# Sliding windows by DMA on one Trainium2 core: a twelfth staged batch, 32 KB packets everywhere, and engine groups set a quarter turn apart

## The chip, the cores and the metric

The kernel runs on one core of one Trainium2 chip. It uses no compute engine for its work: it only moves data with the core's 16 DMA engines. The metric is the device time of one execution in microseconds (us); lower is better. Times are medians of several runs. Ratios are the mean time of one kernel's fast runs over the mean of the other's of the same rounds on the same chip, so a ratio is not quite the ratio of the medians quoted beside it.

## The reference, cut to what matters

```python
batch, length, dim = (32, 4096, 256)      # x: float32, 134 MB
window_size, stride = 64, 32              # so n_windows = 127
for i in range(n_windows):
    start = i * stride
    result[:, i] = x[:, start:start + window_size].copy()
```

Call 32 rows of `x` (32 KB) a *block*. A batch has 128 blocks, and window `i` is block `i` followed by block `i+1`. Nearly every block is therefore written twice. The output is 266.3 MB.

## The kernel before

There are two ways to make a batch of output.

- *Direct*: one DMA copies from `x` in HBM to the output in HBM. Each output byte goes through a DMA engine once, and costs HBM one read and one write (by the page below, 174.83 MB direct counted twice and 138.41 MB staged counted once make 488.07 MB, and HBM read and wrote 488.04 MB).
- *Staged*: a batch's 128 blocks are loaded into SBUF, one block per partition, and stored from there twice. The load is an extra pass through the DMA engines (4.19 MB per batch), but HBM is read only half as often.

The kernel before stages every third batch (11 of 32). Direct work goes out on the queue of the sync engine (`ring_d`, q1 in the profile), staged work on the queue of the scalar engine (`ring_s`, q10), and leftovers of the direct batches (15 windows each, the *edges*) at the end on the software ring of GpSimd (`ring_r`, q0).

```python
DIRECT, IN, OUT = 32768, 16384, 16384       # largest packet, in bytes
...
    def load(self, q, g):                   # class Staging; 6 tiles in SBUF
        ...
        parts = [(k, 4, 32, 1) for k in range(4)] if g == 0 else [(0, step, n, step)]
        for rows in parts:                  # (first partition, step, how many, unit)
            self.issue(self.c.load(q, self.tiles[i], b, c, rows), self.loaded[i])

    def store(self, q, g):
        ...
        parts, end = [((0, step, n, step), 0), ((0, step, n, step), 1)], []
...
    staged = [*range(1, B, 3)]
...
        for i, (b, w) in enumerate(sixteens):       # direct work, 16 windows at a time
            ...                                     # one or two DMAs, by a running share
            count(c.windows(ring_d, b, w, 16), sem)
        ring_r.wait_ge(near, 16)                    # direct queue nearly done
        for b, w, n in edges:
            for k in (b - 1, b + 1):
                if k in place and b != last:
                    st.wait_stored(ring_r, place[k])
            count(c.windows(ring_r, b, w, n), rest)
        count(c.columns(ring_r, last, 116, 9), rest)
```

One DMA is spread over the engines, and each engine takes packets from the queues in turn: the packet records name no engine, but chained end to start, wherever only one chain fits, 99% of the packets in 60-560 us of this kernel's trace are of another queue than the packet before them. What matters is the *turn*: a data packet is one, and so is the four-byte packet at the end of each DMA that counts its semaphore (the 204 direct DMAs of this kernel left 3264 of these in the trace, 16 each). The share of the direct queue is thus set by how many turns in a queue carry data and how long the packets are.

## Time and profile before

| | before |
|---|---|
| time, median of 3 runs | 744.34 us |
| span of the profiled execution | 749.4 us |
| bytes through the DMA engines | 313.26 MB |
| HBM read and written | 220.95 + 267.09 MB |

These are lines of the page of the kernel before: the busy share of the DMA engines in 40 slices (in tenths), what they moved in each slice, the packets, and for each queue its packets, MB and share of the engines' span.

```profile
...
DMA  8999999999999999999999999999999999999996
GB/s 360 401 427 429 427 429 428 434 423 418 420 424 423 418 424 415 422 427 427 414 427 417 429 432 429 430 422 430 429 423 421 423 421 419 425 426 423 431 409 262
DMA packets 18290, 313.26 MB, mean 418 GB/s; under 512 B 4336, under 2 KB 4336, under 8 KB 4528
...
q1 hardware_dynamic: 8016, 154.32, 48.8%
q10 hardware_dynamic: 9104, 138.41, 44.0%
q0 software_dynamic: 1168, 20.51, 6.5%
...
HBM read 220.95 MB, written 267.09 MB: 651 GB/s over the span
...
```

The engines are busy from the second slice to the last but one. The time can only fall if fewer bytes pass, if packets get faster, or if start and end get shorter. The next lines are stretches of the same trace (columns: stretch, its length, GpSimd's busy time, clock, DMA share, GB/s): batches being loaded, then two stretches in which they are stored, then the hand-over from the direct queue to the software ring.

```profile
...
30.00:120.00 90.00, 0.00 (x0) 1.00 1.01 427
150.00:400.00 250.00, 0.00 (x0) 1.00 1.00 422
530.00:650.00 120.00, 0.00 (x0) 1.00 1.01 422
650.00:660.00 10.00, 5.61 (x10) 1.00 0.99 421
...
```

Loading runs at 427 GB/s and storing at 422. The trace's record of each packet shows how far that is from the best: a 32 KB packet takes 1213 ns in the median (1211 at the least), which is called undisturbed below. The mean of the direct queue in this trace is 1236 ns. Staged 16 KB packets take 611 ns undisturbed and 624 on average. Packets that follow each other overlap by 3 to 4 ns in the records, so undisturbed 32 KB packets start 1209 ns apart. That is 27.1 GB/s per engine and 433.6 GB/s for 16, the best rate in what follows.

### The profile page before, as it was taken

The page shows a single profiled execution, that of the slowest core. Times are in us where ns is not written, and L with a number is a line of the kernel's source. Part 1 is how long each engine was busy: PE and PEld are TensorE (multiplying, and loading weights), DVE is VectorE, ACT ScalarE, POOL GpSimd, SP SyncE. Part 2 cuts the span into 40 slices and gives each one's busy share as a digit, 9 for nine tenths or more (in the row PEclk, how much of TensorE's full clock was granted, in tenths as well). Part 3 has the DMA queues.
Part 4 walks back from the last instruction along what each step waited for, and adds up shares of the span by engine and source line. Part 5 has one row for each costly group of instructions (what it writes and reads, how often), then busy time and mean ns, then how long its engine had stood idle before and what let it go on. Part 6 is the DMA issues. An engine that isn't in the chain of part 4 may idle for free.

```text
span 749.4 us, 322 instructions
## 1 busy us (share of the span) xinstructions
POOL 12.8 (2%) x26
## 2 busy tenths in 40 slices
POOL 0000000000000000000000000000000000040100
DMA  8999999999999999999999999999999999999996
GB/s 360 401 427 429 427 429 428 434 423 418 420 424 423 418 424 415 422 427 427 414 427 417 429 432 429 430 422 430 429 423 421 423 421 419 425 426 423 431 409 262
DMA packets 18290, 313.26 MB, mean 418 GB/s; under 512 B 4336, under 2 KB 4336, under 8 KB 4528
## 3 DMA queue, kind: packets, MB, share of 16 engines
q1 hardware_dynamic: 8016, 154.32, 48.8%
q10 hardware_dynamic: 9104, 138.41, 44.0%
q0 software_dynamic: 1168, 20.51, 6.5%
q14 instruction: 2, 0.02, 0.0%
HBM read 220.95 MB, written 267.09 MB: 651 GB/s over the span
## 4 chain that ended last, share of the span: by engine, by line
another core or an unknown queue 92%; POOL 2%; issue 0%; POOLq 0%; SPq 0%
POOL out_dram L34 2%; POOL out_dram L44 0%; POOLq L236 0%; SPq L172 0%; POOLq L114 0%
## 5 line engine op out<-in xcount | busy, mean ns | idle before, releaser
L34 POOL DMA_DIRECT2D out_dram<-in_x_dram x21 | 12.0, 576 | 691.3 <-DMA out_dram<-in_x_dram 654.0
L44 POOL DMA_DIRECT2D out_dram<-in_x_dram x1 | 0.6, 581 | 0.0
L222 POOL MEMSET const-float32-0.0<- 128x1 f32 x1 | 0.1, 98 | 0.2 <-issue 0.2
L222 POOL MEMSET const-bfloat16-1.0<- 128x1 bf16 x1 | 0.1, 101 | 0.0
L222 POOL MEMSET const-float32-1.0<- 128x1 f32 x1 | 0.1, 98 | 0.0
L222 POOL MEMSET const-uint8-127<- 128x1 uint8 x1 | 0.1, 98 | 0.0
## 6 DMA issues: line engine op xcount, KB each, us to landing
out_dram<-in_x_dram SPq DMA_DIRECT2D x92, 1024.0 KB, 100.7
out_dram<-xb ACTq DMA_DIRECT2D x21, 4096.0 KB, 139.7
out_dram<-in_x_dram SPq DMA_DIRECT2D x110, 512.0 KB, 90.3
xb<-in_x_dram ACTq DMA_DIRECT2D x10, 4096.0 KB, 131.4
out_dram<-in_x_dram POOLq DMA_DIRECT2D x20, 960.0 KB, 38.5
xb<-in_x_dram ACTq DMA_DIRECT2D x4, 1024.0 KB, 15.7
out_dram<-xb ACTq DMA_DIRECT2D x2, 1024.0 KB, 113.4
out_dram<-xb ACTq DMA_DIRECT2D x4, 512.0 KB, 96.9
```

The costliest lines, as they stand in the source:

```text
L34: return q.dma_start(out=self.oap((b * self.nw + w0) * 2 + h, [[2 * blk, n], row]), in_=self.xap(b * self.nb + w0 + h, [[blk, n], row]), m ...
L44: return q.dma_start(out=self.oap((b * self.nw + w0) * 2, [[part, 16], [2 * self.blk, n], row]), in_=self.xap(b * self.nb + w0, [[part, 16 ...
L222: nc = _bacc.Bacc("TRN2", target_bir_lowering=False, num_devices=1)
```

## The change

The intent, in the words it came with: "As few long packets: 12 staged batches, all 32 KB, share 0.52 throughout; groups of 4 engines set a quarter turn apart by the software ring".

```diff
-DIRECT, IN, OUT = 32768, 16384, 16384
+DIRECT, IN, OUT, REST = 32768, 32768, 32768, 32768
...
+    def quarters(self, q, b, w0, p0, n):      # 4 windows, meant for 4 engines; n quarters of a turn each
+    def many(self, q, b, w0, n, half):        # 16 engines x n packets of 32 KB, one semaphore
...
-        parts = [(k, 4, 32, 1) for k in range(4)] if g == 0 else [(0, step, n, step)]
-        for rows in parts:
+        for rows in self.split(2):
...
+    def split(self, parts):
+        return [(k, parts, 128 // parts, 1) for k in range(parts)]
...
-        parts, end = [((0, step, n, step), 0), ((0, step, n, step), 1)], []
+        split = self.split(8 if g >= len(self.items) - 4 else 2)
+        parts, end = [(rows, half) for half in (0, 1) for rows in split], []
...
-    staged = [*range(1, B, 3)]
+    staged = [0, 3, 6, 9, 11, 14, 17, 20, 22, 25, 28, 31]
...
+        for k in range(3):
+            count(c.quarters(ring_r, apart[0], apart[1] + 4 * k, 0, 3 - k), rest)
         st.run(ring_s)
...
+        for i, (b, w, n, half) in enumerate(main):
+            count(c.many(ring_d, b, w, n, half), near if i == len(main) - 2 else done)
...
         ring_r.wait_ge(near, 16)
+        for k, p in ((3, 0), (0, 3), (1, 2), (2, 1)):
+            count(c.quarters(ring_r, apart[0], apart[1] + 4 * k, p, 4 - p), rest)
```

`split(2)` is two DMAs of 64 rows (every second partition): 4 data packets and a semaphore packet per engine. A direct `many` is 7 data packets and one semaphore packet. So of two queues that take turns the direct one has 0.875 / (0.875 + 0.8) = 0.52 of the bytes. `split(8)`, used for the stores of the last four batches, is eight DMAs of 16 rows, every eighth partition: one data packet per engine and one semaphore packet.

More of the change, by code (lines that the diff above doesn't have):

```diff
@@ L37, in windows @@
             max_dma_last_dim=piece,
+        )
+    def quarters(self, q, b, w0, p0, n):
+        part = self.blk // 4
+        at = p0 * 2 * part
+        dims = [[n * part, 2], [1, n * part]]
+        return q.dma_start(
+            out=bass.AP(self.out.tensor, self.oap((b * self.nw + w0) * 2, dims).offset + at, [[2 * self.blk, 4], *dims]),
+            in_=bass.AP(self.x.tensor, self.xap(b * self.nb + w0, dims).offset + at, [[self.blk, 4], *dims]),
+            max_dma_last_dim=4 * n * part,
+        )
+    def many(self, q, b, w0, n, half):
+        return q.dma_start(
+            out=self.oap((b * self.nw + w0) * 2 + half, [[2 * self.blk, 16], [32 * self.blk, n], [1, self.blk]]),
+            in_=self.xap(b * self.nb + w0 + half, [[self.blk, 16], [16 * self.blk, n], [1, self.blk]]),
         )
@@ L87, in load @@
         i = g % len(self.tiles)
-        b, c, n = self.items[g]
         if self.count[self.stored[i]]:
             q.wait_ge(self.stored[i], self.count[self.stored[i]])
-        step = 128 // n
-        parts = [(k, 4, 32, 1) for k in range(4)] if g == 0 else [(0, step, n, step)]
-        for rows in parts:
-            self.issue(self.c.load(q, self.tiles[i], b, c, rows), self.loaded[i])
+        for rows in self.split(2):
+            self.issue(self.c.load(q, self.tiles[i], *self.items[g], rows), self.loaded[i])
         self.after_load[g] = self.count[self.loaded[i]]
+    def split(self, parts):
+        return [(k, parts, 128 // parts, 1) for k in range(parts)]
     def store(self, q, g):
         i = g % len(self.tiles)
-        b, c, n = self.items[g]
         q.wait_ge(self.loaded[i], self.after_load[g])
-        step = 128 // n
-        parts, end = [((0, step, n, step), 0), ((0, step, n, step), 1)], []
+        split = self.split(8 if g >= len(self.items) - 4 else 2)
+        parts, end = [(rows, half) for half in (0, 1) for rows in split], []
         if g == len(self.items) - 1:
-            parts = [((0, 1, 128, 1), 1), ((0, 1, 32, 1), 0)]
-            end = [(96, 1, 32, 1)] + [(32 + k, 4, 16, 1) for k in range(4)]
+            parts = [(rows, 1) for rows in split] + [(split[0], 0)]
+            end = split[1:]
         for rows, half in parts:
-            self.issue(self.c.store(q, self.tiles[i], b, c, rows, half), self.stored[i])
+            self.issue(self.c.store(q, self.tiles[i], *self.items[g], rows, half), self.stored[i])
         for rows in end:
-            self.issue(self.c.store(q, self.tiles[i], b, c, rows, 0), self.ended)
+            self.issue(self.c.store(q, self.tiles[i], *self.items[g], rows, 0), self.ended)
         self.after_store[g] = self.count[self.stored[i]]
@@ L140 @@
     c = Copier(x, out, B, L, D, W, S, n_win)
-    staged = [*range(1, B, 3)]
-    items = [(b, -1 if b == B - 1 else 0, c.nb) for b in staged]
-    place = {b: g for g, (b, _, n) in enumerate(items) if n == c.nb}
+    staged = [0, 3, 6, 9, 11, 14, 17, 20, 22, 25, 28, 31]
+    items = [(b, 1 if b == 0 else -1 if b == B - 1 else 0) for b in staged]
+    place = {b: g for g, b in enumerate(staged)}
     direct = [b for b in range(B) if b not in staged]
@@ L157, in count @@
         total[sem] += 16
-    sixteens = []
+    main, edges, singles = [], [], [(B - 1, c.nw - 1, 1)]
+    if 0 in staged:
+        singles.append((0, 0, 0))
+    last = B - 2
     for b in direct:
-        w = 15 if b - 1 in staged else 0
-        sixteens += [(b, w + 16 * j) for j in range((c.nw - w) // 16)]
-    singles = [(B - 1, c.nw - 1, 1)]
-    edges = [(b, 0 if b - 1 in staged else 112, 15) for b in direct[:-1]]
-    last = B - 2
-    edges.append((last, 112, 4))
-    first_loads, loads, stores = 6 * 17, 5 * 17, 6 * 34
-    turns = share = 0
+        before, behind = b - 1 in staged, b + 1 in staged
+        w = 15 if before and (not behind or b == last) else 8 if before else 0
+        if b == last:
+            w = 0
+        main += [(b, w + 16 * j, min(7, 7 - j), half) for j in range(0, 7, 7) for half in (0, 1)]
+        if b == last:
+            edges.append((b, 112, 3))
+        elif before and behind:
+            edges += [(b, 0, 8), (b, 120, 7)]
+        else:
+            edges.append((b, 0 if before else 112, 15))
+    b, w, n, half = main.pop()
+    main += [(b, w, n - 1, half), (b, w + 16 * (n - 1), 1, half)]
+    apart = main[-2][:2]
+    main = [(b, w + 16, n - 1, half) if (b, w) == apart else (b, w, n, half) for b, w, n, half in main]
     with tc.tile_critical():
+        for k in range(3):
+            count(c.quarters(ring_r, apart[0], apart[1] + 4 * k, 0, 3 - k), rest)
         st.run(ring_s)
-        for i, (b, w) in enumerate(sixteens):
-            sem = near if i == len(sixteens) - 2 else done
-            second = turns - first_loads - stores
-            loading = turns < first_loads or 0 <= second < loads
-            share += 120 if turns < 16 or -8 <= second < 16 else 90 if loading else 18
-            if share >= 120:
-                share -= 120
-                turns += 4
-                count(c.windows(ring_d, b, w, 16, 0), done)
-                count(c.windows(ring_d, b, w, 16, 1), sem)
-            else:
-                turns += 3
-                count(c.windows(ring_d, b, w, 16), sem)
-            if i == len(sixteens) // 2:
+        for i, (b, w, n, half) in enumerate(main):
+            count(c.many(ring_d, b, w, n, half), near if i == len(main) - 2 else done)
+            if i == len(main) // 2:
                 for b, w, half in singles:
@@ L196 @@
                     st.wait_stored(ring_r, place[k])
-            count(c.windows(ring_r, b, w, n), rest)
-        count(c.columns(ring_r, last, 116, 9), rest)
+            count(c.windows(ring_r, b, w, n, None, REST), rest)
+        count(c.columns(ring_r, last, 115, 10), rest)
         st.wait_stored(ring_d, place[B - 1])
```

## The prediction

> **What bounds the kernel now.** The 16 DMA engines. The page's DMA row is at 9 in 38 of 40 slices, the stretches from 20 to 720 us show a DMA share of 1.00, and the three queues together hold 99.3% of the engines' span (48.8 + 44.0 + 6.5). So the time is bytes per engine over its best rate, plus a cost per packet, plus slow packets, start and tail.
>
> By the trace's packet records a 32 KB packet takes 1213 ns at best and 1236 on average (direct queue); a staged 16 KB packet 611 at best, 624 on average.  [...] Summed over the best time of their kind, packets lose about 15 us per engine (6.6 direct, 7.0 staged, 1.3 software ring). About 0.5 to 0.9% while batches are loaded (about 40-120 and 415-520 us, direct share of the bytes 0.53), 2.2% while they are stored (150-400 and 530-650 us, share 0.57), 2.5 to 3% in the last 80 us, more in the first 30 us, where all engines go in step (up to 16 direct packets at once). Within the store stretches the loss rises with the direct share: about 1% or less at 0.52, over 4% above 0.62. Direct packets load HBM twice[...].
>
> **What the change does.**
> - Adds one staged batch in place of a direct one: 4.19 MB more through the engines (about 313.3 to 317.5 MB, +1.36%). [...]+9.7 us, wholly on the critical path.
> - Removes half of the staged packets: 872 data packets per engine become about 606. With fewer semaphore packets about 2 us saved (packets overlap by 3-4 ns).
> - Moves the direct share of the store stretches from 0.57 to 0.52. Estimate from the loss by share: 2.2% to about 0.8% over roughly 350 us, 4 to 5 us saved; the load stretches stay.
> - But the last four batches are stored one packet per two turns, so the direct share there is about 0.64, then 0.57 beside the software ring: 100 to 150 us where 2 to 3% stay.
> - The quarter turns break the step at the start; jitter breaks it after about 50 us anyway: at most 2 us.
>
> Sum: about +2 us; if steady share and phases take nearly all the loss away, about -6. The profiled run is some 7 us longer than the timed ones, so part of the loss may exist only there. Middle: 742.5 us.
>
> **What would show it.** After: about 317.5 MB, near 9,700 data packets, direct and staged packets all 32 KB; store stretches with mean packets nearer 1213 ns (about 1222) and 425 to 430 GB/s instead of 422; engines in direct packets at once near 8, with little spread from 20 us on; last 100 us unchanged or worse.
>
> **What would make it wrong.** Lower: loss vanishes everywhere (floor about 737). Higher: [...]equal packets keep engines in step for the whole run; engines end unevenly because the pieces are longer.
>
> Predicted 742.5 us, 735 to 751 in 8 of 10; faster by over 2% 0.02, within 2% 0.94, slower 0.04.

The sum came to about +2 us: +9.7 for the bytes (4.19 MB at the 433.6 GB/s measured above give the same), less 2 for packets, less 4 to 5 for the share, less at most 2 for the quarter turns. The middle, 742.5 us, lies between this +2 and the -6 of the better case. Of the "jitter" the trace of before shows this much: the standard deviation of the number of engines in direct packets at once falls from 6.9 in the first 10 us to 3.3 in 50-60 us.

## More of the kernel before

Last, lines of the timeline (columns: start, time until the last of them, queue, line, operation, names, how many). They show the end: when the direct queue is nearly done, the software ring sends 18 edges at once, and three more after it has waited for stores.

```profile
...
431.72 222.98 ACTq L63 DMA_DIRECT2D out_dram<-xb  x15
654.39 10.26 POOL L34 DMA_DIRECT2D out_dram<-in_x_dram  x18 [653.95 <-DMA out_dram<-in_x_dram]
702.01 1.72 POOL L34 DMA_DIRECT2D out_dram<-in_x_dram  x3 [37.36 <-DMA out_dram<-xb]
...
```

## The result, and the profile after

| | before | after |
|---|---|---|
| time, median of 5 runs | 744.34 us (743.5 to 745.25) | 763.93 us (762.73 to 765.84) |
| ratio, 95% interval | | 1.0265 (1.0247 to 1.0283) |
| span of the profiled execution | 749.4 us | 760.9 us |
| bytes through the DMA engines | 313.26 MB | 317.54 MB |
| HBM read and written | 220.95 + 267.09 MB | 216.86 + 267.19 MB |

The change is slower by 2.65%, outside the predicted range. The lines of its page that answer to those of before:

```profile
...
DMA  8999999999999999999999999999999999999995
GB/s 365 436 427 434 434 431 427 429 438 432 434 427 439 429 429 434 436 436 427 427 427 431 434 438 429 433 432 429 434 436 407 412 413 415 266 402 403 425 409 245
DMA packets 13313, 317.54 MB, mean 417 GB/s; under 512 B 3400, under 2 KB 3400, under 8 KB 3624
...
q10 hardware_dynamic: 6528, 151.00, 47.6%
q1 hardware_dynamic: 5216, 145.95, 44.8%
q0 software_dynamic: 1568, 20.58, 6.6%
...
HBM read 216.86 MB, written 267.19 MB: 636 GB/s over the span
...
```

Up to slice 30 (570 us) this looks better than before: all slices from the second on are at 427 to 439 GB/s. Then come four slices at 407 to 415, one at 266, and five that reach 425 at most. Yet the DMA share stays at 9 tenths: the engines are not idle there, their packets are slow. The stretches (columns as above):

```profile
...
30.00:560.00 530.00, 0.00 (x0) 1.00 1.00 432
560.00:640.00 80.00, 0.00 (x0) 1.00 1.00 415
640.00:680.00 40.00, 13.32 (x23) 1.00 0.99 333
646.00:658.00 12.00, 10.72 (x19) 1.00 1.01 265
...
```

The steady part runs at 432 GB/s. From 560 us it is 415, and around 650 us it is 265 GB/s with all engines busy. The timeline lines of the end:

```profile
...
386.99 277.66 ACTq L81 DMA_DIRECT2D out_dram<-xb  x72
644.55 2.40 POOL L45 DMA_DIRECT2D out_dram<-in_x_dram  x4 [641.05 <-DMA out_dram<-in_x_dram]
646.96 9.76 POOL L34 DMA_DIRECT2D out_dram<-in_x_dram  x17
669.03 1.16 POOL L34 DMA_DIRECT2D out_dram<-in_x_dram  x2 [12.31 <-DMA out_dram<-xb]
712.50 1.71 POOL L34 DMA_DIRECT2D out_dram<-in_x_dram  x3 [42.31 <-DMA out_dram<-xb]
...
```

From 386.99 us on the staged stores are issued. At 644.55 the software ring begins, with the four closing quarter pieces first, then 17 edges. Between 646 and 658 us the packet records show almost only staged packets in flight, with means of 1.6 to 2.7 us in two-microsecond steps, up to 2.2 times the undisturbed 1.21 us.

**Two traces of one chip.** The first profile of before was long (its profiled run took 751.2 us, its timed runs 744 to 745). Profiled again in two later jobs, on two chips, its spans were 744.1 and 743.8; yet another chip took 752 us for the same kernel (below). So the account is made from two traces of one chip, taken side by side: before with a span of 743.8 us, the change with 762.8. First the kernel before, then the change:

```profile
...
0.00:30.00 30.00, 0.20 (x4) 1.00 0.93 385
30.00:560.00 530.00, 0.00 (x0) 1.00 1.01 428
560.00:640.00 80.00, 0.00 (x0) 1.00 1.01 427
640.00:680.00 40.00, 10.26 (x18) 1.00 1.01 429
680.00:720.00 40.00, 2.30 (x4) 1.00 1.01 425
...
```

```profile
...
0.00:30.00 30.00, 2.14 (x7) 1.00 0.94 389
30.00:560.00 530.00, 0.00 (x0) 1.00 1.00 432
560.00:640.00 80.00, 0.00 (x0) 1.00 1.00 410
640.00:680.00 40.00, 13.34 (x23) 1.00 0.99 337
680.00:720.00 40.00, 2.27 (x4) 1.00 1.01 415
...
```

"Lost" below is the length of a stretch less the time that the bytes in it (by the packet records) take at 433.6 GB/s, the best rate measured above. The expectations count it against a rate 0.4% higher, so their losses are larger by 0.4% of the stretch (120-560 us: 11.1 and 3.5 us there, 9.5 and 1.9 here). Share is the direct part of the bytes.

| stretch, us | before: share, lost | change: share, lost | difference |
|---|---|---|---|
| all bytes at the best rate | 722.3 us | 732.2 us | +9.9 |
| 0-30 | 0.55, 3.7 | 0.50, 3.6 | -0.1 |
| 30-560 | 0.56, 7.4 | 0.52, 2.2 | -5.2 |
| 560-640 | 0.58, 1.3 | 0.62, 4.1 | +2.8 |
| 640-680 | 0.51, 0.5 | 0.36, 8.9 | +8.4 |
| 680-720 | 0.58, 0.9 | 0.53, 2.1 | +1.2 |
| 720 to the end | 0.63, 7.7 | 0.55, 9.7 | +2.0 |
| sum | | | +19.0 |

The steady part does what it was built for. Its gain is half of the added bytes, and from 560 us on nearly three times the gain is lost (14.4 us). The gain has two parts. In 30-560 us the packets' time over the best of their kind (1213 and 611 ns) fell from 5.1 to 1.5 us per engine, so 3.6 us come from fewer slow packets; the other 1.6 us come from fewer packets (817 per engine before, 526 after, semaphore packets included).

### The profile page after: what moved, and what is told of

It reads as the page before. It is cut to its first block, busy times and chain, and to the rows that moved or that the text cites. A ratio compares the mean times of both kernels' runs of the same rounds, so it can differ in the third digit from the quotient of the medians.

```text
span 760.9 us, 252 instructions
## 1 busy us (share of the span) xinstructions
POOL 17.7 (2%) x34
## 2 busy tenths in 40 slices
DMA packets 13313, 317.54 MB, mean 417 GB/s; under 512 B 3400, under 2 KB 3400, under 8 KB 3624
## 3 DMA queue, kind: packets, MB, share of 16 engines
HBM read 216.86 MB, written 267.19 MB: 636 GB/s over the span
## 4 chain that ended last, share of the span: by engine, by line
another core or an unknown queue 91%; POOL 2%; issue 0%; PEldq 0%
POOL out_dram L34 1%; POOL out_dram L45 1%; POOL out_dram L62 0%; PEldq L261 0%
## 5 line engine op out<-in xcount | busy, mean ns | idle before, releaser
L45 POOL DMA_DIRECT2D out_dram<-in_x_dram x7 | 4.3, 622 | 642.2 <-DMA out_dram<-in_x_dram 641.0
L34 POOL DMA_DIRECT2D out_dram<-in_x_dram x22 | 12.6, 577 | 54.6 <-DMA out_dram<-xb 54.6
L62 POOL DMA_DIRECT2D out_dram<-in_x_dram x1 | 0.6, 553 | 0.0
```

The costliest lines, as they stand in the source:

```text
L34: return q.dma_start(out=self.oap((b * self.nw + w0) * 2 + h, [[2 * blk, n], row]), in_=self.xap(b * self.nb + w0 + h, [[blk, n], row]), m ...
L45: return q.dma_start(out=bass.AP(self.out.tensor, self.oap((b * self.nw + w0) * 2, dims).offset + at, [[2 * self.blk, 4], *dims]), in_=bas ...
L62: return q.dma_start(out=self.oap((b * self.nw + w0) * 2, [[part, 16], [2 * self.blk, n], row]), in_=self.xap(b * self.nb + w0, [[part, 16 ...
```

## The experiments

The theories: **A**, the 16-row stores of the last four batches are at fault, because they raise the direct share and because rows at step 8 are slow to move by themselves. **B**, the closing quarter pieces on the software ring hold the direct work back. **C**, the added bytes or the 32 KB packets as such. The chips differ from job to job, so kernels of different jobs are best compared by their ratios.

| run | edit | median, us | before beside it | ratio (95% interval) |
|---|---|---|---|---|
| e1_two | last stores in 2 parts | 757.83 | 745.02 | 1.0169 (1.0152-1.0185) |
| e2_four | last stores in 4 parts | 758.05 | 745.02 | 1.0167 (1.0143-1.0191) |
| e3_qlast | closing quarters last | 763.94 | 745.02 | 1.0247 (1.0225-1.0270) |
| e5_nostag | e1_two, no quarters | 757.94 | 745.60 | 1.0168 (1.0150-1.0186) |
| e6_early | e1_two, ring released earlier | 757.24 | 745.60 | 1.0162 (1.0136-1.0189) |
| e7_early4 | e6_early, last two in 4 parts | 756.03 | 745.60 | 1.0140 (1.0125-1.0155) |
| e8_halves | e1_two with halves of SBUF | 775.59 | 745.60 | 1.0407 (1.0388-1.0427) |
| before_again | none | 745.73 | 745.42 | 1.0003 (0.9986-1.0020) |
| e9_loads4 | 32-row loads | 761.49 | 745.42 | 1.0208 (1.0187-1.0229) |
| e10_eleven | 11 batches, share 0.567 | 751.09 | 745.42 | 1.0071 (1.0056-1.0086) |
| e11_half | 32-row loads in the second half | 760.73 | 752.24 (slower chip) | 1.0108 (1.0070-1.0147) |
| e12_loads2 | e10_eleven, 64-row loads | 755.89 | 752.24 (slower chip) | 1.0043 (1.0017-1.0069) |
| e13_half_again | e11_half on another chip | 754.81 | 746.02 | 1.0119 (1.0096-1.0142) |

### The patterns by themselves (e4_ports)

All work of the kernel is replaced by loads and stores on one queue, pattern after pattern, with a full wait between; the result is wrong.

```diff
+        go(stores([(k, 2, 64, 1) for k in range(2)], (0, 2)))
+        go(stores([(k, 8, 16, 1) for k in range(8)], (4, 6)))
+        go(stores([(k, 4, 32, 1) for k in range(4)], (8, 10)))
+        go(stores([(32 + k, 4, 16, 1) for k in range(4)], (12, 14, 16, 18)))
...
```

> A measurement by itself, its result is wrong on purpose: one queue alone, one pattern after another with a full wait between. Loads of 128 rows in 2 parts (step 2), twice, in 8 parts (step 8), in 4 parts (step 4); then stores of 2 batches each: 64 rows step 2; 16 rows step 8; 32 rows step 4; 16 rows step 4 from row 32; 128 rows; 16 rows step 8 in the order 0,4,1,5,2,6,3,7; 32 rows step 1. Theory A: stores of 16 rows at step 8 take near 2.4 us a 32 KB packet[...], 64 rows at step 2 and 16 rows at step 4 from 32 take 1.21 us. Rival (the slow packets at 646-666 us come from something else that goes on then, such as the software ring's descriptors): all patterns 1.21 us.

Mean packet time of 32 KB, and the rate, for each pattern in the packet records:

```
load  64 rows step 2 (twice)               1291, 1285 ns   393, 384 GB/s (start and end included)
load  16 rows step 8                       2474 ns         204 GB/s
load  32 rows step 4                       1286 ns         391 GB/s
store 64 rows step 2                       1221 ns         427 GB/s
store 16 rows step 8, order 0,1,2,...      2311 ns         219 GB/s
store 32 rows step 4                       1222 ns         426 GB/s
store 16 rows step 4, from row 32          1226 ns         419 GB/s
store 128 rows                             1221 ns         427 GB/s
store 16 rows step 8, order 0,4,1,5,...    1675 ns         305 GB/s
store 32 rows step 1                       2351 ns         215 GB/s
```

Stretches inside five of them: the load of 16 rows at step 8, then stores of 64 rows step 2, 16 rows step 8, 32 rows step 4, 16 rows step 4 from row 32:

```profile
...
28.00:47.00 19.00, 0.00 (x0) 1.00 0.95 197
63.00:81.00 18.00, 0.00 (x0) 1.00 1.02 437
84.00:121.00 37.00, 0.00 (x0) 1.00 0.94 213
124.00:142.00 18.00, 0.00 (x0) 1.00 1.02 437
146.00:164.00 18.00, 0.00 (x0) 1.00 1.03 437
...
```

The DMA share is near 1 in all (0.94 to 1.03), and the rate halves for step 8. (A stretch counts whole every packet that starts in it; hence shares above 1 and 437 GB/s in stretches as short as these.) Which rows are moved together decides: 16 rows take 2311 ns a packet at step 8 and 1226 at step 4 from row 32; 32 rows take 2351 ns at step 1 and 1222 at step 4. So neither the number of rows in a part nor the packet size tells fast from slow. The same step-8 parts in the order 0,4,1,5 get part of the rate back. What makes some sets of rows slow is shown by no run. The rival, that something else slowed the packets at 646-666 us, isn't needed. Another rival is the HBM side, because the addresses in the output change with the row pattern: rows at step 8 lie 512 KB apart there. The table speaks against it: 32 neighbouring rows, only 64 KB apart, are as slow as step 8, and the same step-8 parts in another order are faster (305 against 219 GB/s).

### Last stores in 2 or in 4 parts (e1_two, e2_four)

```diff
-        split = self.split(8 if g >= len(self.items) - 4 else 2)
+        split = self.split(2)                                          # e1_two
+        split = self.split(4 if g >= len(self.items) - 4 else 2)       # e2_four
```

> One edit: the last four batches are stored in 2 parts of 64 rows like the others, not 8 parts of 16 rows. Theory A (the 16-row stores are the cause: they raise the direct share to about 0.63 from 570 us on, and alone [...]2.4 us a packet instead of 1.21): the stretch 570-670 us loses its excess, staged packets alone stay near 1.21 us, and the time falls from 764 to 740-748 us. Theory B (the software ring's closing quarter pieces hold direct work back at 645-665 us and starve the engines of it): a stretch of 15-20 us with staged packets alone remains after the direct queue's end, and the time stays at 757 or more. Theory C (32 KB packets as such, or the 1.36% more bytes): 758-764 us.

> One edit: the last four batches in 4 parts of 32 rows (step 4) instead of 8 of 16. Theory A: the direct share there is about 0.57 [...]so most of the loss goes: 742-752 us, between the 2-part run and the change. If the part count alone raised the share[...], the gain over the change would be 3-5 us only (759-761 us). Theory B and C: 760 us or more.

Stretches of e1_two:

```profile
...
560.00:640.00 80.00, 0.00 (x0) 1.00 1.00 432
640.00:680.00 40.00, 14.38 (x25) 1.00 1.01 427
720.00:740.00 20.00, 0.00 (x0) 1.00 1.01 333
...
```

The slow stretch at 640-680 us is gone (427 GB/s, where the change has 333), and so is the loss at 560-640 (0.2 us). But only 6 us (7 by the ratios) came of the 16 or more that A had promised. Staged packets now run fast alone at 658-678 us (1231 ns on average in 640-680 us), finish early (at 712 us), and leave almost 40 us in which only direct packets run: 333 GB/s in 720-740 us, at 1.59 us a packet. At two HBM accesses per byte that is 2 x 333 = 666 GB/s of HBM traffic. e2_four ends the same way. So A is right about the slow packets, but the slow stores had also kept the staged work from finishing too early: taking them away turned one loss into another. The marks that had been set for B beforehand (some 20 us of staged packets alone, 757 us or more) are met by this run; whether the pieces are the reason is what the next two runs ask.

### The quarter pieces (e3_qlast, e5_nostag)

```diff
# e3_qlast: the same four pieces, moved behind the edges
+        for k, p in ((3, 0), (0, 3), (1, 2), (2, 1)):
+            count(c.quarters(ring_r, ...), rest)
         count(c.columns(ring_r, last, 115, 10), rest)
# e5_nostag: e1_two, and no quarters at the start or the end; main takes their 16 windows
```

> One edit: the four closing quarter pieces are issued after all edges instead of before them; 16-row stores stay. Theory A: the direct work is back within 3-5 us of the direct queue's end, so the stretch with staged packets at 2.4 us shrinks from about 20 us to 3-6 us, but the 16-row stores' 4-5% loss at share 0.63 stays: 752-758 us. Theory B: all of the loss of that stretch is gone and the time is 745-750 us. Theory C: 762-765 us.

> Edits: 2 parts for the last four batches (as in e1_two), and no quarter turns: no pieces on the software ring at the start or before the edges, the 16 windows go to the direct queue. Two questions. What does the stagger give in the steady stretch: if it is what keeps the packets at 1213 ns there, the loss of 25-560 us rises from about 0.2% to 2% or more (10 us or more lost, up to 16 engines in direct packets at once throughout); if the share of 0.52 does it, the loss stays under 0.5%. What do the closing quarters cost: without them the direct work is back within 4-8 us of the direct queue's end instead of 20, so about 3 MB less direct work is left to run alone at the end (there a direct packet took 1.49 us instead of 1.21), which gives 3 us. Share theory: 751-756 us. Stagger theory: 762 us or more.

With the pieces last, the slow stretch became shorter (lost in 640-680 us: 5.9 us, 9.1 in the first trace of the change), but the pieces then stood at the end, where staged packets were slow instead (1.4 to 1.9 us in 740-752 us; 12.5 us lost from 720 us on, against 8.6). The time did not move. So this run shows only that moving the pieces moves the loss; my own number for A (752 to 758) was missed, and so was B's (745 to 750).

e5_nostag asks what the quarter turn gives. Its stretches:

```profile
...
30.00:560.00 530.00, 0.00 (x0) 1.00 1.00 431
720.00:740.00 20.00, 0.00 (x0) 1.00 1.01 336
...
```

Its steady stretch runs at the rate of the change, though its packet records show the engines much more in step (standard deviation of the number of engines in direct packets at once in 60-90 us: 5.7, against 3.2 in the change). The ratio to before equals e1_two's (1.0168 and 1.0169). So the quarter turns give nothing measurable; the direct share of 0.52 is enough. Taking out the closing pieces did not help either: the time, 757.94 us, is that of e1_two and missed the 751 to 756 expected. With e4_ports, in which the packets are slow without any pieces, this rules B out as the cause of the slow packets.

### The rows alone (e8_halves)

```diff
-        split = self.split(8 if g >= len(self.items) - 4 else 2)
+        split = self.split(2)
+        if g >= len(self.items) - 4:
+            split = [(0, 1, 64, 1), (64, 1, 64, 1)]
```

> e1_two with one difference: the last four batches' two parts are rows 0-63 and 64-127 instead of even and odd rows. Turns, packets, semaphores and shares are those of e1_two; only the SBUF partitions that are read together differ[...]. [...]staged packets from about 570 us on rise well above 1213 ns, to 1.5-2.4 us where they run alone, the direct share rises with that, and the time is 8-20 us above e1_two (766-778). Rival (the loss of the change came from the share and from the number of semaphores alone): equal to e1_two, 757-759 us.

Turns, packets and semaphores are those of e1_two, only the partitions differ, and the time is 17 to 18 us higher (775.59 against 757.83, from two jobs; ratios 1.0407 and 1.0169). Its stretches, to be read against e1_two's 432 and 427 GB/s:

```profile
...
560.00:640.00 80.00, 0.00 (x0) 1.00 1.00 413
640.00:680.00 40.00, 13.34 (x23) 1.00 1.01 382
...
```

Mean staged packets in 640-680 us took 1415 ns here and 1231 in e1_two. The choice of rows alone can cost this much, beside direct work too. One part of the expectation failed: the direct share did not rise (0.52 in 560-640 us in both), and yet 3.6 us of these 80 were lost, where e1_two lost 0.2. The change lost 4.1 us there.

### Trying to balance the end (e6_early, e7_early4, e9_loads4, e11_half, e13_half_again)

If the direct work that is left alone at the end is what costs, it should be given turns earlier.

```diff
# e6_early: e1_two, with
-            count(..., near if i == len(main) - 2 else done)
+            count(..., near if i == len(main) - 3 else done)     # and the closing quarters after ten edges
# e7_early4: e6_early, with
+        split = self.split(4 if g >= len(self.items) - 2 else 2)
# e9_loads4: e7_early4 without quarters, with
-        for rows in self.split(2):
+        for rows in self.split(4):                               # loads: share 0.57
# e11_half and e13_half_again: e9_loads4, with
+        for rows in self.split(4 if g >= 6 else 2):
```

> Edits over e1_two: the software ring is released one direct transfer earlier (about 12 us) and the four closing quarters go out after ten edges instead of first. Theory (what e1_two still loses is imbalance: staged packets alone for 20 us after the direct queue's end, therefore direct packets alone for 40 us at the end, at 1.49 us each): the stretch of staged packets alone goes, the direct packets alone shrink from 40 to 15-25 us, time 749-754 us. Rival (the slow direct packets at the end come from the edges' addresses or from the software ring itself): they stay at 1.4-1.5 us also beside staged packets, and the time stays at 757-758.

> e6_early and the last two batches in 4 parts of 32 rows, so that staged packets take 2 turns of 3 like the edges do and both end together. Theory of balance: direct packets alone at the end under 10 us, 744-750 us, 3-5 us below e6_early. Rival: the share rises early and costs as much as it saves, equal to e6_early within 1.5 us.

> e7_early4 without the quarter pieces, and with the loads in 4 parts of 32 rows, so that the direct share is 0.57 while batches are loaded and about 5 MB of direct work moves from the end into the load stretches. Theory of balance (what is left over 744 us is direct work that runs alone at the end, at 1.5 to 1.6 us a packet): the stretch of direct packets alone falls from 24 us to under 10, and the time from 756 to 748-751 us. Rival (12 staged batches can't be balanced better[...]): 755-757 us.

> e9_loads4 with 32-row loads only for the second six batches; the first six in 2 parts of 64 rows again. e7_early4 (all loads in 2 parts) ended with 24 us of direct packets alone, e9_loads4 (all in 4) with staged packets left over, so this should end near balance. Theory (bytes decide: +9.8 us for the twelfth batch, 4 to 4.6 us saved by the steady share of 0.52, end as good as before's): 750 to 754 us, not below 749. Rival (something else in the 12-batch kernel costs several us, for instance 32-row parts beside the edges at 660-720 us): 755 us or more, with the loss of the stretches before 640 us still under 8 us.

> e11_half unchanged, on another chip, because its first chip ran everything slower (the kernel before took 752.2 us there, 745 elsewhere). Bytes theory: 1.007 to 1.011 of the kernel before, that is 750 to 754 us where before takes 745. End theory (a balanced end is all that was missing): 1.00 or less.

e6_early missed: the hand-over became smooth (427 GB/s in 640-680 us), but at 706-712 us the software ring had little in flight again, now with its quarter pieces (the mean of its packets there is 707 ns, so most are shorter than 32 KB), and direct packets still ran alone from about 720 us. Without any quarters (e5_nostag) the end was no better. e7_early4 gained 1 us at most: the intervals overlap, as its rival (equal within 1.5 us) had it. e9_loads4 missed on the other side: the 32-row loads cost 2 us in 30-120 us (2.2 lost, 0.2 in e7_early4) and 3.3 us in 350-560, and staged work was left at the end. Between the two, e11_half ended near balance: direct packets alone only around 742-748 us. Its chip ran everything slower (before took 752.24 us there, in 7 runs of 751.0 to 754.3, and 744 to 746 us on the others), so it was repeated as e13_half_again: 754.81 us, ratio 1.0119, just above what the bytes theory said (1.007 to 1.011; the interval reaches down to 1.0096) and far from the end theory's 1.00. In its trace 22.2 us are lost, nearly what before loses beside it (21.5); what stays are the 9.9 us of bytes. Its stretches show the slow spot gone:

```profile
...
560.00:640.00 80.00, 0.30 (x1) 1.00 1.00 433
640.00:680.00 40.00, 10.40 (x19) 1.00 1.00 426
680.00:720.00 40.00, 2.21 (x4) 1.00 1.01 414
...
```

### Long packets without the twelfth batch (before_again, e10_eleven, e12_loads2)

```diff
# e10_eleven: the change without quarters, ring released as in e6_early, and
-    staged = [0, 3, 6, 9, 11, 14, 17, 20, 22, 25, 28, 31]
+    staged = [*range(1, B, 3)]
+        for rows in self.split(4):              # loads, and stores likewise
# e12_loads2: e10_eleven, with
+        for rows in self.split(2):              # loads
```

> The kernel before, unchanged, profiled and timed beside itself: its first profile had a span of 749.4 us and a profiled run of 751.2 us while its timed runs took 744 to 745. If that profile was a slow look, a new one has a span near 743 us and its store stretches lose less than 2.2%; then a part of the gain of the steady stretch (120-560 us: 11.1 us lost before, 3.5 after) is not real. If profiling costs it 5 us each time, the span is again 748-750. Ratio of times 1.00 within 0.3%.

> The long packets without the twelfth batch: 11 staged batches as before, all packets 32 KB, loads and stores in 4 parts of 32 rows (2 data packets of 3 turns) against 7 of 8, so a direct share of 0.567 throughout; no quarter pieces; the software ring's edges as before. Theory (long packets and a steady share remove most of the slow packets also at 0.56 to 0.57, and the twelfth batch's 4.3 MB are a cost of 9.8 us for nothing): the steady stretch loses under 1.5%, both kinds of work end together, 736-741 us, faster than both kernels. Rival[...]: the loss stays at 2 to 3% in the store stretches and the time at 744-748 us.

> e10_eleven with the loads in 2 parts of 64 rows: direct share 0.52 while batches are loaded, 0.567 while they are stored, which is nearly the distribution of the kernel before (0.53 and 0.57), but with 32 KB packets. Theory (the share alone sets the loss; packet length gives nothing): the load stretch 30-120 us loses about 1 us as in before instead of 2.5, the store stretch 120-350 us 4 to 5.5 us as in both; some 4 MB of direct work are left for the end; 747 to 751 us. If long packets do help at an equal share, 120-350 us loses under 3.5 us and the time is below 744 us.

before_again settles that the first profile of before was slower than usual: here its span is 744.1 us, and its packets lose 8.3 us per engine over their best times, not 15.

e10_eleven was meant to beat both kernels and does not: 751 us, more even than its rival's 744 to 748. Its steady stretch:

```profile
...
30.00:560.00 530.00, 0.00 (x0) 1.00 1.00 424
...
```

On the same chip it loses 12.1 us in 30-560 us, before_again 6.2. In the stores alone (120-350 us) it is 4.6 us at a share of 0.56 against 3.4 at 0.57 (4.0 in before's trace from another chip, e14_before_beside). So long packets do not lower the loss; here it is rather higher, by one trace of each. e12_loads2 has the lower share while loading, but fell on the slower chip, and left direct packets alone at the end (13.8 us lost from 720 us on). Its 6.9 us lost in 120-350 us can't be set against a trace of before from that chip, since there is none; the ratio, 1.0043, is not below 1. No version was found that beats the kernel before.

### Two traces of one chip (e14_before_beside, e15_after_beside)

> The kernel before, for a trace on the same chip as the two others. Time as its timed runs; loss of about 8 us in 30-560 us on a usual chip, 13 us on a chip like the first.

> The change, for a trace on the same chip. Against before beside it: +9.8 us of bytes, 4 us less lost in 30-560 us, about 2 us more in 560-640 us, 8 to 9 us more in 640-680 us; sum 16 to 18 us of span.

Single runs of 745.62 and 764.53 us. They gave the table by stretch above. All its rows came out near what was expected: +9.9 of bytes, -5.2 in 30-560 us, +2.8 in 560-640, +8.4 in 640-680; the sum of 19.0 us is a little over the expected 16 to 18.

## Why the prediction was wrong

- **"Adds one staged batch": +9.7 us on the critical path.** Right: 9.9 us.
- **"Moves the direct share ... 4 to 5 us saved".** Right in sign, and a little too high: of the 5.2 us gained in 30-560 us on one chip, 3.6 come from fewer slow packets. The 15 us of loss it started from were too high, though: 8.3 to 9.0 us on the chips that before was profiled on again. So the lower part of the range, "the loss vanishes everywhere", did not exist.
- **"With fewer semaphore packets about 2 us saved".** Nearly right: the other 1.6 us of the gain, with 620 data packets per engine where the prediction had 606.
- **"The quarter turns ... at most 2 us".** Right as a bound: without them the ratio is the same (1.0168 and 1.0169).
- **"But the last four batches are stored one packet per two turns, so the direct share there is about 0.64, then 0.57 ...: 100 to 150 us where 2 to 3% stay".** This is the step that failed. The first half of it was under-sized: in 560-640 us the share was 0.62 and the loss 4.1 of 80 us, 5.2%. The prediction itself had read over 4% above a share of 0.62 in the trace of before, and did not use it here. How much of the 4.1 us comes from the share and how much from the rows is not told apart: e8_halves lost 3.6 us there by its rows at a share of 0.52. The second half was not what happened: from 646 us on there was hardly any direct work for some 20 us, staged packets ran nearly alone, and at step 8 they took 1.6 to 2.7 us. The stretch of 640-680 us lost 8.9 us of 40, where before lost 0.5.
- **A row pattern as a danger.** The forecast named the 64-row loads with step 2 among the dangers, and did not expect it to come true. The right kind of danger at the wrong place. Rows at step 2 are clean (stores take 1221 ns a packet); the 16-row stores at step 8 of the same diff, which I had read only for their turns, are not (2311 ns alone). A run of each row pattern of the diff by itself, as in e4_ports, would have shown it.
- **The end.** I assumed the end to be as before. It lost 3.2 us more from 680 us on, and e1_two shows that without the slow stores it would still not have been balanced.

Without the failed step the change would have come nearer to the forecast: with 9.9 of bytes, 5.2 saved, and the end of before, to 4.7 us over before, near 749 us (742.5 were predicted). That is an estimate from the table, and no run reached it; the nearest (e13_half_again) is at 1.0119, which is 753 us where before takes 744.34. So two things are to be kept apart. The slow end was the larger part of the slowdown, and a flaw that can be mended (ratio 1.0265 with it, 1.0119 in e13_half_again); the plan itself, bytes against share, is shown by no run to pay.

**An estimate of why it can't pay much.** HBM traffic is the engines' rate times (1 + share): 418 x 1.558 = 651 GB/s over the whole of before, as its page says. In stretches that lose time it comes out alike: 427 x 1.58 = 675 GB/s (before, 560-640 us), 424 x 1.57 = 666 (e10_eleven), 333 x 2 = 666 (direct alone in e1_two; 336 and 340 x 2 = 672 and 680 in e5_nostag and e7_early4). (The change in 560-640 us has 410 x 1.62 = 664, but there the rows took part.) Take 670 as a limit; that HBM is what holds these packets up is an inference from this likeness, and no trace shows it. The engines' best is 433.6, as measured above; the steady part of the change reached 432. By these two numbers they meet at a share of 670/433.6 - 1 = 0.545. With 11 batches (needed share about 0.56) HBM would limit: 488.0 MB / 670 = 728 us. With 12 (0.52) the engines would: 317.5 MB / 433.6 = 732 us. By this estimate the kernel before, at 0.56, already sat close to where the two limits cross.

**What stays open.** In e1_two, e2_four and e9_loads4 packets were 4 to 6% slow at 660-720 us (in e1_two until 712 us) beside the edges, at a share under 0.5 and with rows that were fast in e4_ports (1221 and 1222 ns); no run tells why. Whether long packets at an equal share are really worse, or e10_eleven's lack of variation is, was not told apart.

## What to carry to other kernels

When a DMA is split into parts, time the row pattern of each part by itself: a step that divides the work evenly over the engines can still double the packets (2311 ns at step 8, 1221 at step 2), and it did not show as idle time but as busy engines (DMA share 0.94 in e4_ports). When two kinds of transfer share the engines, count the turns of each queue to the very end, for what is left of one kind runs alone at its own rate (333 GB/s for direct packets in e1_two), and removing a slow spot may only move the loss there. Before buying less of one resource with more of another, estimate both limits from traces: by the estimate above, the kernel before already stood close to where they cross.
